# Transposing the attention probabilities: from TensorE to 32x32 blocks on VectorE

## The chip, the cores and the metric

The kernel runs on one core of one Trainium2 chip. The metric is the device time of one execution in microseconds. Three runs of the kernel before took 821.98, 822.05 and 822.8 us, median 822.05 us. The execution that the profiler recorded took 822.53 us; its span from the first to the last instruction is 820.8 us.

## What is computed

Two decoder layers over 256 positions of width 2048, with float32 inputs and outputs. Layer 0 mixes by multi-scale pooling, layer 1 by block-sparse causal attention (12 heads of 128; with 256 positions and blocks of 256 it is plain causal attention over one block). Both layers also attend over 256 memory tokens with 4 heads:

```python
s = einsum('bshd,bmhd->bhsm', q, k) * (HEAD_DIM ** -0.5)
p = softmax(s, axis=-1)
mem_o = einsum('bhsm,bmhd->bshd', p, v)
...
y = concat([branch * silu(gate_b), mem_o * silu(gate_m)]) @ w_out[i]
h = layer_norm(alpha * h + y)
```

The softmax runs along the keys. Its rows are computed with positions on the partitions and keys along the free dimension; the product with the values sums over keys, and TensorE sums over partitions. So each block of probabilities has to be transposed between the two.

## The kernel before

Every large product is split in two: each float32 operand x becomes `hi` (x in the float32r type) and `lo` (x minus hi), and a product is the sum of hi*hi, hi*lo and lo*hi. ScalarE makes the hi part (L71), VectorE the lo part (L72), in the helper `split`.

The program is one long list of items. An item is one block of weights, 128 x 1024 (512 KB), with the matmuls that consume it. `run` (L130) goes through the list: at item i it issues `prep` of item i+3 (`wh` on ScalarE, then `wl` on VectorE), then the load of item i+4 (on SP's queue), then the matmuls of item i, then whatever was registered with `later` for that item. There are four buffers of `wh`/`wl` (W_BUFS) and four of `raw` (RAW_BUFS). The engines run their queues in order, and every queue has the order in which this loop issues. A product of 256 columns is four items (`proj_t`); at the end of the fourth, `done` folds the accumulators on ScalarE and VectorE (L220, L221), and for queries and keys it adds a cast and a subtraction for each half (L228, L229).

Attention is computed for two heads at a time: `MemPair` for the memory (two pairs in each layer, 4 in all) and `MobaPair` for the causal attention (two pairs in each of three groups of four heads, 6 in all). A pair has these steps, which `plan` (L380) registers at distances in items, counted from the item that ends the query projection (called item 0 below):

- `a`: the scores on TensorE into the PSUM tile `s2`; VectorE adds the mask (causal only, L350) and takes the row maxima (L266, L267).
- `exps`, one item later: ScalarE's exponentials with row sums, into tile `p` (L271).
- `divide`, two items after `a`: the reciprocal and four multiplications by it on VectorE, in place (L275, L277).
- `b(0)` and `b(1)`, one for each head: TensorE transposes the 128x128 blocks of `p` into the PSUM tile `pt` (four blocks for the memory, L312; three for the causal pair, L362), and `split` makes `ph` and `pl` from `pt`.
- `c`: the products with the values into `o`; then `gated` (L282) multiplies by the gate and splits into `zT`, the input of the output projection.

The memory pairs use plan(1, 5, 9) and plan(7, 11, 14): item numbers of `a`, of `b(0)` and of `c`. The causal pairs use plan(1, 5, 17) and plan(7, 18, 20). Items 1 to 8 are the gate projection. In layer 1, items 9 to 16 behind the memory's gates are the keys of the first causal group; in layer 0 they are the first pooling inputs. In a causal group items 9 to 16 are the value projection.

Of the kernel before, what the change touches and what calls it, by code (L numbers as in the profile page):

```python
# [11 lines left out]
F32 = mybir.dt.float32  # L12
# [5 lines left out]
P = 128  # L18
T = 256
# [13 lines left out]
BLK = 1024  # L33
RAW_BUFS = 4
WARM = 10
SHIFT = 40
W_BUFS = 4
SHIFT = 40
LD = 4
# [6 lines left out]
def trunk(ctx: ExitStack, tc: tile.TileContext, a: dict, out: bass.AP):  # L46
    nc = tc.nc
    ctx.enter_context(tc.manual_schedule())
    sb = ctx.enter_context(tc.tile_pool(name="sb", bufs=1))
    ps = ctx.enter_context(tc.tile_pool(name="ps", bufs=1, space=bass.MemoryType.PSUM))  # L50
# [5 lines left out]
    KX = KT * 2 * T  # L56
    xT, memT = (xm[:, SHIFT + i * KX:SHIFT + (i + 1) * KX].rearrange("p (k t) -> p k t", k=KT) for i in range(2))
    kept = [xm[:, i * KX:(i + 1) * KX].rearrange("p (k n) -> p k n", k=KT) for i in range(2)]
    zT = sb.tile([P, KT, 2 * T], F32R, name="zT")
    res = sb.tile([P, 2, D], F32, name="res")  # L60
    ident = mask = psc = eps_t = stats = None

    f = lambda ap: ap.bitcast(F32)

# [1 line left out]
    def mm(o, l, r, start, stop):  # L66
        nc.tensor.matmul(o, l, r, start=start, stop=stop)  # L67

    def split(hi, lo, src):

        nc.scalar.activation(hi, src, AF.Copy)  # L71
        nc.vector.tensor_sub(lo, src, f(hi))  # L72
# [19 lines left out]
    def later(n, fn):  # L92
        events[now[0] + n].append(fn)
# [158 lines left out]
    def heads_tile(name):  # L252
        return sb.tile([P, 4, 2 * T], F32R, name=name)


    class Rows:
# [17 lines left out]
        def divide(self):  # L274
            nc.vector.reciprocal(self.sm, self.sm)  # L275
            for c, (src, dst) in enumerate(self.rows):
                nc.vector.tensor_scalar_mul(dst, dst, self.sm[:, c:c + 1])  # L277

    def gated(o, g, kt):

        zf = sb.tile([P, T], F32, name="zf", bufs=3)
        nc.vector.scalar_tensor_tensor(zf, o, 0.5, g, op0=ALU.mult, op1=ALU.mult)  # L282
        split(zT[:, kt, :T], zT[:, kt, T:], zf)

    class MemPair(Rows):
# [3 lines left out]
        def a(self):  # L289
            q, k = self.st["q"], self.st["k"]  # L290
            s = ps.tile([P, 2, 2, T], F32, name="s2")
            for j in range(2):
                h = self.h0 + j
                for t in range(2):
                    qh = q[:, h, t * P:(t + 1) * P]
                    ql = q[:, h, T + t * P:T + (t + 1) * P]
                    mm(s[:, j, t], qh, k[:, h, :T], True, False)
                    mm(s[:, j, t], qh, k[:, h, T:], False, False)
                    mm(s[:, j, t], ql, k[:, h, :T], False, True)
            self.p = p = sb.tile([P, 2, 512], F32, name="p")  # L300
            p4 = p.rearrange("p j (t m) -> p j t m", t=2)
            self.rows = [(s[:, j, t], p4[:, j, t]) for j in range(2) for t in range(2)]
            self.maxima([(0, 4, s)])

        def b(self, j):
            if j == 0:
                self.ph = sb.tile([P, 2, 512], F32R, name="ph")
                self.pl = sb.tile([P, 2, 512], F32R, name="pl")
            pt = ps.tile([P, 512], F32, name="pt")
            for m in range(2):  # L310
                for t in range(2):
                    nc.tensor.transpose(pt[:, m * T + t * P:m * T + (t + 1) * P],  # L312
                                        self.p[:, j, t * T + m * P:t * T + (m + 1) * P], ident)
            split(self.ph[:, j], self.pl[:, j], pt)

        def c(self):
            v, g = self.st["v"], self.st["g"]
# [13 lines left out]
    class MobaPair(Rows):  # L331
# [5 lines left out]
        def a(self):  # L337
            q, k = self.st["q"], self.st["k"]
            s = ps.tile([P, 2, 512], F32, name="s2")
            for j in range(2):  # L340
                h = self.h0 + j
                for t, (c0, w) in enumerate(((0, P), (P, T))):
                    qh = q[:, h, t * P:(t + 1) * P]
                    ql = q[:, h, T + t * P:T + (t + 1) * P]
                    d = s[:, j, c0:c0 + w]
                    mm(d, qh, k[:, h, :w], True, False)
                    mm(d, qh, k[:, h, T:T + w], False, False)
                    mm(d, ql, k[:, h, :w], False, True)
            self.p = p = sb.tile([P, 2, 512], F32, name="p")
            nc.vector.tensor_tensor(p[:, :, :384], s[:, :, :384],  # L350
                                    mask[:, None, :].to_broadcast([P, 2, 384]), op=ALU.add)

            self.rows = [(p[:, j, c0:c1],) * 2 for c0, c1 in ((0, P), (P, 384)) for j in range(2)]
            self.maxima([(0, 2, p[:, :, :P]), (2, 4, p[:, :, P:384])])

        def b(self, j):
            if j == 0:
                self.ph = sb.tile([P, 2, 512], F32R, name="ph")
                self.pl = sb.tile([P, 2, 512], F32R, name="pl")
            pt = ps.tile([P, 512], F32, name="pt")  # L360
            for c in range(3):
                nc.tensor.transpose(pt[:, c * P:(c + 1) * P], self.p[:, j, c * P:(c + 1) * P], ident)  # L362
            split(self.ph[:, j, :384], self.pl[:, j, :384], pt[:, :384])

        def c(self):
            v, g = self.st["v"], self.st["g"]
# [13 lines left out]
    def plan(pr, a, b, c):  # L380

        later(a, pr.a)
        later(a + 1, pr.exps)
        later(a + 2, pr.divide)
        later(b, lambda: pr.b(0))
        later(b + 1, lambda: pr.b(1))
        later(c, pr.c)
# [21 lines left out]
    def load_gb(n):  # L409
        gb = []  # L410
        for nm in ("ln_g", "ln_b"):
            tl = sb.tile([P, 512], F32, name=nm, bufs=2)
            src = a[nm][0, n * 512:(n + 1) * 512]
            nc.sync.dma_start(tl, src[None, :].to_broadcast([P, 512]))
            gb.append(tl)
        return gb
# [13 lines left out]

    def constants():

        nonlocal ident, mask, psc, eps_t, stats
        ident = sb.tile([P, P], F32, name="ident")
        mask = sb.tile([P, 384], F32, name="mask")
        psc = sb.tile([P, 12], F32, name="psc")
        eps_t = sb.tile([P, 48], F32, name="eps_t")
        stats = sb.tile([P, 2, 5, 6], F32, name="stats")
        nc.vector.memset(eps_t[:, 0:1], EPS)
        nc.scalar.dma_start(ident, a["ident"])  # L440
        nc.scalar.dma_start(mask, a["mask"])
        for g in range(2):
            inv.append(sb.tile([P, 2, T], F32, name="ln_g", bufs=2))
            nc.scalar.dma_start(inv[g], a["inv"][None, 2 * g:2 * g + 2].to_broadcast([P, 2, T]))
        nc.scalar.dma_start(psc, a["pool_scale"])

        def prepare():
            nc.vector.tensor_scalar_mul(psc, psc, 0.5)
            for z in (U0, U1, S0, S1):
                nc.vector.memset(z[:, :, :PAD], 0.0)  # L450
        later(20, prepare)
# [4 lines left out]
    def fresh(key, make):  # L456

        tiles = []

        def g():  # L460
            if not tiles:
                tiles.append(make())
                st[key] = tiles[0]
            return tiles[0]
        return g
# [16 lines left out]
    def w_in(layer, c):  # L482
        return [a["w_in"][layer, c, kb] for kb in range(4)]
# [12 lines left out]
    def mem_q_gate(layer):  # L496
        q = fresh("q", lambda: heads_tile("qq"))
        g = fresh("g", gate_tile)
        for c in range(2):
            proj_t(xT, w_in(layer, 12 + c), to_heads(q, 2 * c))  # L500
        prs = [MemPair(0, st), MemPair(2, st)]

        def go():
            plan(prs[0], 1, 5, 9)
            plan(prs[1], 7, 11, 14)
        after(go)
        for c in range(2):
            proj_t(xT, w_in(layer, 14 + c), to_gate(g, 2 * c))
# [98 lines left out]
    for half in range(2):  # L607
# [3 lines left out]
        g = fresh("g", gate_tile)  # L611
# [43 lines left out]
    for grp in range(3):  # L655
        k = fresh("k", lambda: heads_tile("kk"))
        q = fresh("q", lambda: heads_tile("qq"))
        g = fresh("g", gate_tile)
        v = fresh("v", val_tile)
        for c in range(2):  # L660
            proj_t(xT, [a["w_sk"][2 * grp + c, kb] for kb in range(4)], to_heads(k, 2 * c))
        for c in range(2):
            proj_t(xT, w_in(1, 2 * grp + c), to_heads(q, 2 * c))
        prs = [MobaPair(2 * j, 4 * grp + 2 * j, st) for j in range(2)]

        def go(prs=prs):
            plan(prs[0], 1, 5, 17)
            plan(prs[1], 7, 18, 20)
        after(go)
        for c in range(2):  # L670
            proj_t(xT, w_in(1, 6 + 2 * grp + c), to_gate(g, 2 * c))
        proj_n(xT, [a["w_sv"][grp, kb] for kb in range(8)], to_values(v), place=in_mem)
# [45 lines left out]
    def with_constants(*w):  # L718
        old(*w)
        constants()  # L720
# [71 lines left out]
    pt = ps.tile([P, 512], F32, name="pt")[:5, :P]  # L792
# [69 lines left out]
```

## Time and profile before

| | |
|---|---|
| runs | 821.98, 822.05, 822.8 us (median 822.05) |
| profiled execution | 822.53 us, span 820.8 us |
| TensorE matmul (PE) | 810.8 us busy, 99% of the span |
| TensorE weight load (PEld, beside PE) | 700.9 us, 85% |
| VectorE (DVE) | 558.5 us, 68%, 794 instructions |
| ScalarE (ACT) | 396.2 us, 48% |
| mean granted TensorE clock | 0.995 of full speed |

How to read it: an engine's busy time is the union of its instructions' time. Matmuls are pipelined, so the recorded length of one is longer than the distance from its start to the next one's start; what a group of them costs TensorE is read from the chain of work that ended last, which gives the time by which each piece moved the end on. The same holds, to a smaller degree, for VectorE and ScalarE: the recorded lengths of two neighbours overlap a little when the second needs nothing from the first.

### The profile page before, as it was taken

What the parts mean: (1) busy time and instruction counts of PE and PEld (TensorE: products, weight loads), DVE (VectorE), ACT (ScalarE), POOL (GpSimd) and SP (SyncE); (2) the same over time, 40 slices, a digit from 0 to 9 for tenths busy, and PEclk for the clock granted to TensorE, in tenths of its full rate; (3) what the DMA queues carried; (4) which work ended last, traced back from release to release, by engine and by line L of the source; (5) the groups of instructions that cost most, each with busy time, mean ns of one, the idle gap of its engine ahead of it and who ended that gap; (6) DMA issues with size and microseconds to landing.
All of it is one profiled execution on the core that took longest, in us unless ns stands there. A gap on an engine that the chain in (4) does not pass through costs nothing.

```text
span 820.8 us, 11537 instructions
## 1 busy us (share of the span) xinstructions
PE 810.8 (99%) x4446; PEld 700.9 (85%) x4446; DVE 558.5 (68%) x794; ACT 396.2 (48%) x578; POOL 0.2 (0%) x4
## 2 busy tenths in 40 slices
PE   9999999999999999999999999999999999999996
PEld 6888888898888888888888888888888888888885
DVE  5786678657956555797667667576765667658746
ACT  6564545545545343545455445354554445545520
POOL 0000000000000000000000000000000000000000
PEclk9999999999999999999999999999999999999998
DMA  8876545456557655676554544645455554636742
GB/s 319 298 250 206 170 154 192 172 181 212 185 190 278 221 186 199 201 234 201 185 170 143 193 162 163 212 159 189 177 173 170 185 187 158 224 113 233 277 132 103
DMA packets 47164, 159.15 MB, mean 194 GB/s; under 512 B 5375, under 2 KB 7167, under 8 KB 46847
## 3 DMA queue, kind: packets, MB, share of 16 engines
q1 hardware_dynamic: 45792, 155.21, 56.3%
q10 hardware_dynamic: 1316, 3.19, 1.0%
q8 instruction: 35, 0.57, 0.3%
q14 instruction: 21, 0.17, 0.1%
HBM read 156.28 MB, written 2.10 MB: 193 GB/s over the span
## 4 chain that ended last, share of the span: by engine, by line
PE 98%; DVE 1%; DMA 1%; SPq 0%; ACT 0%; issue 0%; DVEq 0%
PE acc L67 89%; PE o L67 4%; PE s L67 2%; PE pt L67 2%; DMA raw<-in_w_mk 1%; PE pt L362 0%; PE pt L312 0%; SPq L98 0%; DVE res L805 0%; PE o L637 0%; PE pt L637 0%; DVE res L786 0%; DVE wl L72 0%; ACT wh L71 0%; DVE stats L744 0%
## 5 line engine op out<-in xcount | busy, mean ns | idle before, releaser
L67 PE MATMUL acc<-xm,wh 128*128 128x512 f32 x1344 | 466.8, 394 | 0.5 <-ACT wh L71 0.5
L72 DVE TENSOR_TENSOR wl<-raw,wh 128x1024 fp32r<-128x1024 f32 (+2 forms) x250 | 295.0, 1187 | 149.8 <-ACT wh L71 148.8
L67 PE MATMUL acc<-xm,wl 128*128 128x256 f32 x1344 | 362.6, 280 | 0.1
L71 ACT ACTIVATE wh<-raw 128x1024 fp32r<-128x1024 f32 (+2 forms) x250 | 255.5, 1028 | 188.5 <-PE acc L67 131.2
L67 PEld LDWEIGHTS acc<-xm,wh 128*128 128x128 f32 x1344 | 247.2, 188 | 49.1 <-ACT wh L71 1.0
L67 PEld LDWEIGHTS acc<-xm,wl 128*128 128x128 f32 x1344 | 252.7, 188 | 7.9 <-DVE wl L72 0.9
L67 PE MATMUL acc<-wh,zT 128*128 128x512 f32 x448 | 140.0, 390 | 0.0
L67 PEld LDWEIGHTS acc<-wh,zT 128*128 128x128 f32 x448 | 84.1, 188 | 17.3
L67 PE MATMUL acc<-wl,zT 128*128 128x512 f32 x224 | 87.2, 389 | 0.0
L67 PE MATMUL acc<-xm 128*128 128x512 f32 x288 | 65.8, 389 | 0.0
L67 PEld LDWEIGHTS acc<-xm 128*128 128x128 f32 x288 | 54.1, 188 | 11.2
L72 DVE TENSOR_TENSOR xm<-raw,xm 128x1024 fp32r<-128x1024 f32 (+2 forms) x41 | 47.8, 1171 | 21.1 <-ACT xm L71 21.1
L220 ACT ACTIVATE fold<-acc 128x256 f32<-128x256 f32 x72 | 27.7, 385 | 60.8 <-PE acc L67 59.6
L71 ACT ACTIVATE xm<-raw 128x1024 fp32r<-128x1024 f32 (+2 forms) x41 | 41.3, 1014 | 19.1 <-PE acc L67 9.8
L67 PEld LDWEIGHTS acc<-wl,zT 128*128 128x128 f32 x224 | 42.1, 188 | 8.5
L221 DVE TENSOR_TENSOR fold<-acc,fold 128x256 f32<-128x256 f32 x72 | 29.5, 419 | 4.6 <-ACT fold L220 4.6
L71 ACT ACTIVATE zT<-zf 128x256 fp32r<-128x256 f32 x32 | 12.9, 414 | 39.6 <-DVE zf L282 35.4
L67 PE MATMUL acc<-xm,zT 128*128 128x256 f32 (+1 forms) x144 | 22.6, 318 | 0.0
L67 PEld LDWEIGHTS acc<-xm,zT 128*128 128x128 f32 x144 | 20.7, 190 | 1.9
L67 PE MATMUL acc<-wh,xm 128*128 128x512 f32 x64 | 21.6, 403 | 0.0
L71 ACT ACTIVATE ph<-pt 128x384 fp32r<-128x384 f32 (+1 forms) x20 | 10.7, 535 | 22.2 <-PE pt L362 13.5
L72 DVE TENSOR_TENSOR zT<-zf,zT 128x256 fp32r<-128x256 f32 x32 | 12.9, 423 | 9.7 <-ACT zT L71 9.7
(124 smaller groups left out, 504.4 us busy)
## 6 DMA issues: line engine op xcount, KB each, us to landing
raw<-in_w_in SPq DMA_DIRECT2D x128, 512.0 KB, 3.5
raw<-in_w_out SPq DMA_DIRECT2D x64, 512.0 KB, 4.1
raw<-in_w_sk SPq DMA_DIRECT2D x24, 512.0 KB, 4.4
raw<-in_w_sv SPq DMA_DIRECT2D x24, 512.0 KB, 3.3
raw<-in_w_mv SPq DMA_DIRECT2D x14, 512.0 KB, 5.2
raw<-in_w_mk SPq DMA_DIRECT2D x12, 512.0 KB, 3.4
raw<-in_xT SPq DMA_DIRECT2D x4, 512.0 KB, 4.8
res<-in_x ACTq DMA_DIRECT2D x2, 1024.0 KB, 5.4
```

The source lines that it names most:

```text
L67: nc.tensor.matmul(o, l, r, start=start, stop=stop)
L71: nc.scalar.activation(hi, src, AF.Copy)
L72: nc.vector.tensor_sub(lo, src, f(hi))
L220: nc.scalar.activation(dst, acc[:, T:], AF.Copy)
L221: nc.vector.tensor_add(dst, acc[:, :T], dst)
```

## The change

The transposes leave TensorE. `exps` writes the probabilities into a new tile `ebuf` (called `e`), in an order in which the 32x32 blocks lie as VectorE needs them: the free dimension is cut into four groups g of n blocks of 32 columns (n = 8 for a memory pair, 6 for a causal pair), and group g holds columns 32g to 32g+31 of every 128-wide block. `divide` works on `e` in place. The new method `turn(g)` issues four VectorE transposes; the one for h reads partitions 32h to 32h+31 of group g and writes partitions 32g to 32g+31 of tile `p`, at columns h*32n to (h+1)*32n. One instruction covers 32 partitions and 32n columns: 256 for a memory pair, 192 for a causal pair. `b(j)` is then only the split, from `p` in SBUF instead of from `pt` in PSUM; its operand is read in runs of 32 elements.

`plan` registers turn(0) with `divide` (item a+2, behind it), turn(1) and turn(2) at a+3, turn(3) at a+4. `b(0)` moves from item 5 to 6 in the first pairs and from 11 to 12 in the memory's second pair; that pair's `c` moves from 14 to 15. The two halves of `ebuf` take the place of the two `ln_b` buffers of the first layer norm, so that no memory is added. In the causal pairs `p` holds the masked scores until the exponentials have read them.

```diff
+        def blocks(self, n):
+            self.n = 32 * n
+            self.p = sb.tile([P, 2, 512], F32, name="p").rearrange("p j c -> p (j c)")
+            self.e = ebuf.rearrange("p j c -> p (j c)")[:, :4 * self.n]
+
+        def group(self, t, c0, c1, m):
+            t = t[:, :4 * self.n].rearrange("p (g x) -> p g x", g=4)[:, :, 32 * c0:32 * c1]
+            return t.rearrange("p g (m s) -> p m g s", m=m)
+
+        def turn(self, *groups):
+            for g in groups:
+                for h in range(4):
+                    nc.vector.transpose(self.p[32 * g:32 * g + 32, h * self.n:(h + 1) * self.n],
+                                        self.e[32 * h:32 * h + 32, g * self.n:(g + 1) * self.n])
...
 class MemPair:
-            self.p = p = sb.tile([P, 2, 512], F32, name="p")
-            p4 = p.rearrange("p j (t m) -> p j t m", t=2)
-            self.rows = [(s[:, j, t], p4[:, j, t]) for j in range(2) for t in range(2)]
+            self.blocks(8)
+            e = self.e.rearrange("p (g j m t s) -> p j t m g s", g=4, j=2, m=2, t=2)
+            self.rows = [(s[:, j, t].rearrange("p (m g s) -> p m g s", m=2, g=4), e[:, j, t])
+                         for j in range(2) for t in range(2)]
...
         def b(self, j):
-            pt = ps.tile([P, 512], F32, name="pt")
-            for m in range(2):
-                for t in range(2):
-                    nc.tensor.transpose(pt[:, m * T + t * P:m * T + (t + 1) * P],
-                                        self.p[:, j, t * T + m * P:t * T + (m + 1) * P], ident)
-            split(self.ph[:, j], self.pl[:, j], pt)
+            hi, lo = (t[:, j].rearrange("p (m h s) -> p m h s", m=4, h=4) for t in (self.ph, self.pl))
+            split(hi, lo, self.group(self.p, 4 * j, 4 * j + 4, 4))
...
 class MobaPair:
-            for c in range(3):
-                nc.tensor.transpose(pt[:, c * P:(c + 1) * P], self.p[:, j, c * P:(c + 1) * P], ident)
-            split(self.ph[:, j, :384], self.pl[:, j, :384], pt[:, :384])
+            hi, lo = (t[:, j, :384].rearrange("p (m h s) -> p m h s", m=3, h=4) for t in (self.ph, self.pl))
+            split(hi, lo, self.group(self.p, 3 * j, 3 * j + 3, 3))
...
 def plan(pr, a, b, c):
         later(a + 2, pr.divide)
+        later(a + 2, lambda: pr.turn(0))
+        later(a + 3, lambda: pr.turn(1, 2))
+        later(a + 4, lambda: pr.turn(3))
...
-            tl = sb.tile([P, 512], F32, name=nm, bufs=2)
+            tl = sb.tile([P, 512], F32, name=nm, bufs=2) if nm == "ln_g" else ebuf[:, n % 2]
...
-            plan(prs[0], 1, 5, 9)
-            plan(prs[1], 7, 11, 14)
+            plan(prs[0], 1, 6, 9)
+            plan(prs[1], 7, 12, 15)
...
-            plan(prs[0], 1, 5, 17)
+            plan(prs[0], 1, 6, 17)
             plan(prs[1], 7, 18, 20)
```

## Rows read from the trace of the kernel before

**Rows 1.** The page: busy times of the engines, and the chain that ended last by engine and by line.
```profile
PE 810.8 (99%) x4446; PEld 700.9 (85%) x4446; DVE 558.5 (68%) x794; ACT 396.2 (48%) x578; POOL 0.2 (0%) x4
...
PE 98%; DVE 1%; DMA 1%; SPq 0%; ACT 0%; issue 0%; DVEq 0%
```

**Rows 2.** All waits of TensorE (engine, line, what it waited for: us in total, times, longest).
```profile
PE pt L793 <- DVE cc L790: 2.8, 1, 2.8
PE pt L67 <- DVE zT L125: 1.2, 1, 1.2
PE acc L67 <- ACT wh L71: 0.5, 1, 0.5
PE acc L67 <- ACT cct L795: 0.4, 1, 0.4
```

**Rows 3.** The chain in order of time, memory attention of layer 1 (start us, us, what). Sixteen matmul pairs of an item are 2.78 us.
```profile
411.16 11.12 PE acc L67 x64
422.28 0.44 PE pt L312 x4
422.72 2.78 PE acc L67 x16
425.50 0.44 PE pt L312 x4
425.93 2.78 PE acc L67 x16
428.71 1.44 PE s L67 x12
430.15 5.58 PE acc L67 x32
435.72 1.44 PE o L67 x12
437.16 5.56 PE acc L67 x32
442.72 0.44 PE pt L312 x4
443.16 2.79 PE acc L67 x16
445.95 0.44 PE pt L312 x4
446.39 5.55 PE acc L67 x32
```

**Rows 4.** The same, first causal group.
```profile
496.46 0.33 PE pt L362 x3
496.79 2.78 PE acc L67 x16
```

**Rows 5.** Groups of instructions, shapes apart (count, then busy us and mean ns of one, then idle before).
```profile
L362 PE MATMUL pt<-ident,p 128*128 128x128 f32 x36 | 5.9, 271 | 0.0
L312 PE MATMUL pt<-ident,p 128*128 128x128 f32 x32 | 4.8, 272 | 0.0
L72 DVE TENSOR_TENSOR zT<-zf,zT 128x256 fp32r<-128x256 f32 x32 | 12.9, 423 | 9.7 <-ACT zT L71 9.7
L72 DVE TENSOR_TENSOR wl<-raw,wh 128x384 fp32r<-128x384 f32 x4 | 2.2, 556 | 0.6 <-ACT wh L71 0.6
L277 DVE TENSOR_SCALAR p<-p,sm 128x256 f32<-128x256 f32 x28 | 8.2, 350 | 0.1
```

**Rows 6.** VectorE in order of time, memory attention of layer 1 (start us, us, engine, line, what; in brackets the idle time before it).
```profile
406.31 0.42 DVE L221 TENSOR_TENSOR fold<-acc,fold 128x256 f32<-128x256 f32 x1
406.77 0.29 DVE L228 CAST qq<-fold 128x256 fp32r<-128x256 f32 x1
407.09 0.43 DVE L229 TENSOR_TENSOR qq<-fold,qq 128x256 fp32r<-128x256 f32 x1
407.44 0.42 DVE L221 TENSOR_TENSOR fold<-acc,fold 128x256 f32<-128x256 f32 x1
...
416.92 1.23 DVE L72 TENSOR_TENSOR wl<-raw,wh 128x1024 fp32r<-128x1024 f32 x1 [3.15 <-ACT wh L71]
418.06 0.17 DVE L275 RECIPROCAL sm<-sm 128x4 f32<-128x4 f32 x1
418.27 1.14 DVE L277 TENSOR_SCALAR p<-p,sm 128x256 f32<-128x256 f32 x4
419.32 1.22 DVE L72 TENSOR_TENSOR wl<-raw,wh 128x1024 fp32r<-128x1024 f32 x1
420.46 0.75 DVE L221 TENSOR_TENSOR fold<-acc,fold 128x256 f32<-128x256 f32 x2
421.12 1.22 DVE L72 TENSOR_TENSOR wl<-raw,wh 128x1024 fp32r<-128x1024 f32 x1
...
430.18 1.22 DVE L266 TENSOR_REDUCE nb<-s 128x4 f32<-128x1024 f32 x1 [1.41 <-PE s L67]
431.44 0.17 DVE L267 TENSOR_SCALAR nb<-nb 128x4 f32<-128x4 f32 x1
431.52 1.22 DVE L72 TENSOR_TENSOR wl<-raw,wh 128x1024 fp32r<-128x1024 f32 x1
...
437.31 0.42 DVE L282 SCALAR_TENSOR_TENSOR zf<-o,gate 128x256 f32<-128x256 f32 x1
...
439.80 0.17 DVE L275 RECIPROCAL sm<-sm 128x4 f32<-128x4 f32 x1
...
441.73 2.36 DVE L72 TENSOR_TENSOR wl<-raw,wh 128x1024 fp32r<-128x1024 f32 x2
444.00 0.69 DVE L72 TENSOR_TENSOR pl<-pt,ph 128x512 fp32r<-128x512 f32 x1
```

**Rows 7.** ScalarE in order of time, the same stage: the exponentials of the second pair, from the first to the `wh` behind them, and the one table load before the first pair's.
```profile
412.71 1.28 ACT L271 ACT_TABLE_LOAD   x1 [2.00 <-DVE nb L267]
...
433.26 0.47 ACT L271 ACTIVATE p<-s,nb 128x256 f32<-128x256 f32 x1
...
435.06 1.08 ACT L71 ACTIVATE wh<-raw 128x1024 fp32r<-128x1024 f32 x1
```

**Rows 8.** The page: issues of the load of a weight block (count, KB each, median us from issue to landing).
```profile
raw<-in_w_sk SPq DMA_DIRECT2D x24, 512.0 KB, 4.4
```

More of the change, by code (lines that the diff above doesn't have):

```diff
@@ L35 @@
 WARM = 10
-SHIFT = 40
 W_BUFS = 4
@@ L60, in trunk @@
     res = sb.tile([P, 2, D], F32, name="res")
-    ident = mask = psc = eps_t = stats = None
+    ident = mask = psc = eps_t = stats = ebuf = None
     f = lambda ap: ap.bitcast(F32)
@@ L348, in a @@
                     mm(d, ql, k[:, h, :w], False, True)
-            self.p = p = sb.tile([P, 2, 512], F32, name="p")
+            self.blocks(6)
+            p = self.p.rearrange("p (j c) -> p j c", j=2)
             nc.vector.tensor_tensor(p[:, :, :384], s[:, :, :384],
                                     mask[:, None, :].to_broadcast([P, 2, 384]), op=ALU.add)
-            self.rows = [(p[:, j, c0:c1],) * 2 for c0, c1 in ((0, P), (P, 384)) for j in range(2)]
+            self.rows = [(p[:, j, c0 * P:c1 * P].rearrange("p (m g s) -> p m g s", m=c1 - c0, g=4),
+                          self.group(self.e, 3 * j + c0, 3 * j + c1, c1 - c0))
+                         for c0, c1 in ((0, 1), (1, 3)) for j in range(2)]
             self.maxima([(0, 2, p[:, :, :P]), (2, 4, p[:, :, P:384])])
@@ L359, in b @@
                 self.pl = sb.tile([P, 2, 512], F32R, name="pl")
-            pt = ps.tile([P, 512], F32, name="pt")
-            for c in range(3):
-                nc.tensor.transpose(pt[:, c * P:(c + 1) * P], self.p[:, j, c * P:(c + 1) * P], ident)
-            split(self.ph[:, j, :384], self.pl[:, j, :384], pt[:, :384])
+            hi, lo = (t[:, j, :384].rearrange("p (m h s) -> p m h s", m=3, h=4) for t in (self.ph, self.pl))
+            split(hi, lo, self.group(self.p, 3 * j, 3 * j + 3, 3))
         def c(self):
@@ L431, in constants @@
     def constants():
-        nonlocal ident, mask, psc, eps_t, stats
+        nonlocal ident, mask, psc, eps_t, stats, ebuf
         ident = sb.tile([P, P], F32, name="ident")
@@ L438, in constants @@
         stats = sb.tile([P, 2, 5, 6], F32, name="stats")
+        ebuf = sb.tile([P, 2, 512], F32, name="ebuf")
         nc.vector.memset(eps_t[:, 0:1], EPS)
```

## The prediction

> **What bounds the kernel now.** The page first: TensorE is busy for 99% of the span and is 98% of the chain that ended last, VectorE for 68% [rows 1]. The list of TensorE's waits then shows that this is real: four waits, 4.9 us in all, at the start and the end of the program and none in an attention stage [rows 2]. So whatever leaves TensorE's queue shortens the run, as long as the other engines still deliver in time. The chain in order of time gives what leaves: four memory transposes move the end by 0.44 us, three causal ones by 0.33 us [rows 3, 4], 0.11 us each, though each is recorded with 271 ns [rows 5]. The timeline of VectorE, read last, shows how much room its queue has where the new work goes [rows 6].
>
> **What is removed.** 32 memory transposes in 8 blocks and 36 causal ones in 12 blocks [rows 5]: 8 x 0.44 + 12 x 0.33 = 7.5 us off TensorE.
>
> **What is added: the price.** Each pair issues 16 VectorE transposes, of 256 columns (4 memory pairs) or 192 (6 causal pairs). No row shows one. From below: the divisions, 256 columns each, start every 0.264 us (four last 1.14 us, one 0.35, [rows 6, 5]). The cheapest price for 192 is then 0.23. The nearest rows pass 256 columns once: 423 ns recorded [rows 5]. From 256 to 384 columns it rises by 133 ns, 1.04 ns a column, so 192 columns are 0.357 us. Two such neighbours start 0.35 us apart when the second needs nothing of the first (L229, then L221) and 0.46 when it needs it (L221, then L228) [rows 6]. From above: a second pass of the columns, 0.423 + 0.267 = 0.69 us (0.557 for 192). I take the recorded length, 0.423 and 0.357 us start to start: each transpose reads other partitions than the one ahead of it, so I give it no overlap, and since no data passes between them, no gap either. That is 64 x 0.423 + 96 x 0.357 = 61 us more for VectorE, 68% to about 75% of the span: no bound as a mean. It comes in bursts, though: turn(0) to turn(3) put 6.8 us into three items of 2.78 us in which VectorE has 1.15 us of `wl` each and more besides.
>
> [...]
>
> **What the queue does with it.** An item's `wl` is issued three items ahead, so VectorE may fall some 6 us behind before TensorE waits. I follow VectorE's queue through the memory stage of layer 1, in the clock of [rows 6]; items count from the last query item. A `wl` takes 1.15 us of the queue (start to next start) and is readable 0.1 later.
> First pair: the divisions end at 419.3, turn(0) 421.0, wl(7) and two folds 422.8, turn(1, 2) 426.2, wl(8) 427.4, turn(3) 429.0, two gate products 429.7, wl(9) 430.9 (item 9 starts at 432.06), the two `pl` with wl(10) between them 433.2, maxima 434.5 where they ended at 431.5 before [rows 6]. TensorE has not waited.
> Second pair: wl(11) and two folds to 436.3. ScalarE's exponentials wait for the maxima: 1.8 us [rows 7], then wh(12) until 437.5, so wl(12) ends at 438.6; the gated output 2.5 us (437.31 to 439.80 in [rows 6]) 441.1, reciprocal and divisions 442.4, turn(0) 444.1, gates 444.7, wl(13) 445.9. Item 13 started at 446.39 [rows 3]; four transpose blocks less, it starts at 444.63 and needs wl(13) 0.23 later: it waits 1.1 us. Then turn(1, 2) 449.3, wl(14) 450.4: item 14 waits 1.75 us. Then turn(3), wl(15) 453.3: 0.06. Then two folds with casts and subtractions (2.0 us), `pl`, wl(16), `pl` until 457.6, which `c` needs at 456.7: 0.07 and 1.03. Sum 4.0 us of waits against 1.76 us saved.
> Layer 0 has no table load ahead of its exponentials (1.28 us in layer 1, [rows 7]), so its queue is 1.3 us earlier, and plain folds at item 12: waits of 1.6 us in all against 1.76 saved.
> The causal groups: 5.7 us a pair, no gated output at item 9 and no fold at item 12. The tightest block is wl(14) (same list, 0.2 us in hand): no wait, 3 x 1.32 = 3.96 us saved.
> Sum: -7.5 + 4.0 + 1.6 = -1.8 us. The profiled execution took 822.53 us, so 820.7; it lay 0.48 us over the median of the runs, so against that 820.2.
>
> **Edits at no cost.** `b` splits from SBUF; `pl` costs the same, and `ph` waits for turn(3) in place of TensorE, behind which only `wh` queues, with three items of room. `exps` and `divide` move as many elements as before. The later `c` of the memory's second pair moves TensorE work, it adds none. Loads: SP's next load is released by the late `wl`, up to 4 us later than before, and lands 4.4 us after its issue [rows 8]; its `wh` is due another item later, so ScalarE absorbs that. `ln_b` in `ebuf` is read by the first layer norm, before the second use of `ebuf` begins. Without this cover each would show as a further wait of TensorE of 1 us or so per stage.
>
> **Rivals.**
> *The transposes overlap* like independent neighbours: 0.34 and 0.27 us. For it: no data passes between them. Against: the partitions change at every one. Until wl(13) of the second memory pair 20 transposes have each saved 0.083 us, 1.66 us, more than the 1.1 us that were missing; wl(14) is late by 0.55, the second product by 0.82, layer 0 and the causal groups wait for nothing: -7.5 + 1.4 = -6.1 us, 816.0. With every wait gone, at the bound from below, 814.6.
> *Each pays a gap as well*: the slower side. All sixteen write one tile; if each waits for the one ahead as L228 does for L221, or has a longer fixed part, they start 0.46 us apart or more (0.39 for 192). In layer 1 wl(13) is then 20 x 0.037 = 0.74 us later, wl(14) 0.3 us more: 5.2 us of waits; layer 0 2.8; and the causal wl(14) loses its margin, 0.58 in each group: 5.2 + 2.8 + 1.7 - 7.5 = +2.3, 824.4. At 0.49 and 0.42 the same list gives +6.9, 829. It decides from 0.443 us (0.375) on, where the list's sum is zero: 20 ns over my price.
> *Two passes*, 0.69 and 0.557: the burst no longer fits, and nearly every further microsecond of it is a wait; the list gives +33 us, 855. For it only that the elements are four bytes wide; against it that the other passes of [rows 5] move four bytes at one a step.
>
> [...]
>
> **Chances and range.** Forecast 0.35 (818.5 to 824 by prices of 0.41 to 0.45), overlap 0.33, gap 0.21, two passes or some other large loss 0.11. Less than 0.2% (1.65 us) can't be told from no change here. Faster: all of the overlap and somewhat over a third of the forecast's case, 0.46; within: 0.21; slower: 0.33. The range runs from the overlap's 815 to the gap's 829; only the last case and the ends lie outside.
>
> **What would show it.** TensorE's busy time falls by 7.5 us in any case, and `pt` of L312 and L362 is gone. Right: transposes recorded near 0.42 and 0.36 us, starting as the one ahead ends; waits of TensorE on `wl` (L72) at items 13 and 14 of the memory stages, 1 to 2 us each, and on `pl` in layer 1; none in the causal groups. Overlap: 0.35 us or less start to start, and hardly a wait. Gap: waits on `wl` in the causal groups too. Wrong altogether: waits elsewhere (on `ph`, on a load, on ScalarE), a lower granted clock after the waits, or a `divide` that got slower by its new order of elements.

## The result, and the profile after

The changed kernel took 830.93 us (median of four runs, 830.28 to 831.6) against 822.01 us for the kernel before on the same chip: 1.0107 of its time, 95% interval 1.0094 to 1.0119. It is slower by about 9 us, where 1.8 us faster was forecast and 829 us was the end of the range. The profiled execution's span went from 820.8 to 828.5 us.

The page of the changed kernel, the lines that answer to [rows 1]:

```profile
PE 807.3 (97%) x4378; PEld 693.8 (84%) x4378; DVE 619.5 (75%) x954; ACT 394.8 (48%) x578; POOL 0.2 (0%) x4
...
PE 77%; DVE 17%; ACT 3%; issue 2%; DMA 1%; SPq 0%; DVEq 0%
...
PE acc L66 70%; DVE p L294 6%; DVE wl L71 3%; PE o L66 3%; DVE xm L71 2%; PE pt L66 2%; ACT ebuf L270 2%; PE s L66 1%; DVE ebuf L276 1%; ACT wh L70 1%; DVE gate L241 1%; DVE pl L71 1%; DVE nb L265 1%; DMA raw<-in_w_mk 1%; DVE fold L220 0%
```

TensorE has lost its 68 transposes and is no longer the whole chain: 17% of it now runs through VectorE, the transposes (L294) being the largest part with 6%. All the line numbers are one lower than before up to the new methods (`wl` is L71, `wh` L70).

All waits of TensorE's matmuls, answering to [rows 2]; and the two waits of its weight loads that are new in size (in the kernel before weight loads waited 0.9 us for `wl`, and never for `xm`, the value weights of the causal groups):

```profile
PE acc L66 <- DVE wl L71: 7.0, 4, 2.3
PE acc L66 <- DVE xm L71: 3.9, 3, 1.3
PE pt L812 <- DVE cc L809: 2.8, 1, 2.8
PE pt L66 <- DVE zT L124: 1.2, 1, 1.2
PE acc L66 <- ACT wh L70: 0.6, 1, 0.6
PE acc L66 <- ACT cct L814: 0.4, 1, 0.4
```

```profile
PEld acc L66 <- DVE wl L71: 9.8, 8, 2.8
PEld acc L66 <- DVE xm L71: 7.0, 9, 1.7
```

The second fence is the better account. A matmul is recorded for longer than the distance to the next one's start (a matmul of 512 columns has 394 ns on the page, and the next starts 0.23 us after it), so a wait counted from its recorded end comes out short. 9.8 + 7.0 us less the 0.9 of before are 15.9 us, near what was lost: the span grew by 7.7 and 7.5 us of transposes left TensorE, 15.2 us together.

Where they fall shows in the chain's score matmuls, which open each attention stage. Kernel before, then changed kernel (start us, us, what):

```profile
76.20 1.44 PE s L67 x12
...
409.73 1.44 PE s L67 x12
...
483.95 1.38 PE s L67 x12
...
579.32 1.38 PE s L67 x12
...
674.68 1.38 PE s L67 x12
```

```profile
76.23 1.44 PE s L66 x12
...
411.71 1.44 PE s L66 x12
...
490.42 1.38 PE s L66 x12
...
586.39 1.38 PE s L66 x12
...
682.38 1.38 PE s L66 x12
```

The changed kernel is later by 0.0, 2.0, 6.5, 7.1 and 7.7 us, and by 7.7 at the end. With what each stage saved added back (1.76 us a memory stage, 1.32 a causal group), layer 0's memory stage lost 3.7 us in waits, layer 1's 6.2, the causal groups 1.9, 2.0 and 1.3.

VectorE in the memory stage of layer 1, in order of time, answering to [rows 6], and the price of a transpose from the groups by shape:

```profile
420.04 0.17 DVE L274 RECIPROCAL sm<-sm 128x4 f32<-128x4 f32 x1
420.25 1.14 DVE L276 TENSOR_SCALAR ebuf<-ebuf,sm 128x256 f32<-128x256 f32 x4
421.42 1.77 DVE L294 STREAM_TRANSPOSE p<-ebuf 32x256 f32<-32x256 f32 x4
423.23 1.23 DVE L71 TENSOR_TENSOR wl<-raw,wh 128x1024 fp32r<-128x1024 f32 x1
424.37 0.75 DVE L220 TENSOR_TENSOR fold<-acc,fold 128x256 f32<-128x256 f32 x2
425.15 3.59 DVE L294 STREAM_TRANSPOSE p<-ebuf 32x256 f32<-32x256 f32 x8
428.77 1.23 DVE L71 TENSOR_TENSOR wl<-raw,wh 128x1024 fp32r<-128x1024 f32 x1
430.03 1.80 DVE L294 STREAM_TRANSPOSE p<-ebuf 32x256 f32<-32x256 f32 x4
...
447.88 1.22 DVE L71 TENSOR_TENSOR wl<-raw,wh 128x1024 fp32r<-128x1024 f32 x1
449.13 3.59 DVE L294 STREAM_TRANSPOSE p<-ebuf 32x256 f32<-32x256 f32 x8
452.75 1.23 DVE L71 TENSOR_TENSOR wl<-raw,wh 128x1024 fp32r<-128x1024 f32 x1
```

```profile
L294 DVE STREAM_TRANSPOSE p<-ebuf 32x192 f32<-32x192 f32 x96 | 35.5, 370 | 1.6
L294 DVE STREAM_TRANSPOSE p<-ebuf 32x256 f32<-32x256 f32 x64 | 27.9, 436 | 1.1
```

Eight transposes last 3.59 us: each starts 0.45 us after the one ahead, recorded 0.436 us, so the next begins 0.013 us after the last has ended. There is also a seam, an overlap lost, at both ends of a turn: the division before turn(0) and the transpose before `wl` each run out in full (420.25 + 1.14 = 421.39, next start 421.42; 421.42 + 1.77 = 423.19, next start 423.23), where `wl` and a fold overlap by 0.09 us (423.23 + 1.23 = 424.46, next start 424.37).

### The profile page after: what moved, and what is told of

Its sections match the earlier page's. It is cut to its first block, busy times and chain, and to the rows that moved or that the text cites. A ratio compares the mean times of both kernels' runs of the same rounds, so it can differ in the third digit from the quotient of the medians.

```text
span 828.5 us, 11566 instructions
## 1 busy us (share of the span) xinstructions
PE 807.3 (97%) x4378; PEld 693.8 (84%) x4378; DVE 619.5 (75%) x954; ACT 394.8 (48%) x578; POOL 0.2 (0%) x4
## 4 chain that ended last, share of the span: by engine, by line
PE 77%; DVE 17%; ACT 3%; issue 2%; DMA 1%; SPq 0%; DVEq 0%
PE acc L66 70%; DVE p L294 6%; DVE wl L71 3%; PE o L66 3%; DVE xm L71 2%; PE pt L66 2%; ACT ebuf L270 2%; PE s L66 1%; DVE ebuf L276 1%; ACT wh L70 1%; DVE gate L241 1%; DVE pl L71 1%; DVE nb L265 1%; DMA raw<-in_w_mk 1%; DVE fold L220 0%
## 5 line engine op out<-in xcount | busy, mean ns | idle before, releaser
L71 DVE TENSOR_TENSOR wl<-raw,wh 128x1024 fp32r<-128x1024 f32 (+2 forms) x250 | 294.9, 1187 | 139.0 <-ACT wh L70 138.0
L70 ACT ACTIVATE wh<-raw 128x1024 fp32r<-128x1024 f32 (+2 forms) x250 | 255.0, 1028 | 198.9 <-PE acc L66 130.0
L66 PEld LDWEIGHTS acc<-xm,wl 128*128 128x128 f32 x1344 | 253.5, 189 | 16.8 <-DVE wl L71 9.8
L66 PE MATMUL acc<-xm 128*128 128x512 f32 x288 | 67.9, 394 | 3.9 <-DVE xm L71 3.9
L294 DVE STREAM_TRANSPOSE p<-ebuf 32x192 f32<-32x192 f32 (+1 forms) x160 | 63.4, 396 | 2.7
L71 DVE TENSOR_TENSOR xm<-raw,xm 128x1024 fp32r<-128x1024 f32 (+2 forms) x41 | 47.7, 1169 | 11.6 <-ACT xm L70 11.4
L70 ACT ACTIVATE xm<-raw 128x1024 fp32r<-128x1024 f32 (+2 forms) x41 | 41.1, 1011 | 16.3 <-PE acc L66 6.6
L70 ACT ACTIVATE zT<-zf 128x256 fp32r<-128x256 f32 x32 | 12.9, 415 | 37.9 <-DVE zf L300 33.6
L70 ACT ACTIVATE ph<-p 128x384 fp32r<-128x384 f32 (+1 forms) x20 | 11.1, 557 | 39.5 <-DVE p L294 39.5
```

The source lines that it names most:

```text
L294: nc.vector.transpose(self.p[32 * g:32 * g + 32, h * self.n:(h + 1) * self.n], self.e[32 * h:32 * h + 32, g * self.n:(g + 1) * self.n])
```

## The experiments

The theory after the result: the amount of work that VectorE got is affordable, its place is not. The turns lie in front of `wl` in VectorE's queue, in bursts that its lead of three items can't cover, and a transpose costs 0.45 us because it changes the quarter of partitions. Rivals: the new layouts and the split from SBUF cost the time; a transpose costs what it costs wherever it reads; VectorE has too much to do as a whole.

**The transposes left out.** `turn` does nothing, and the splits read `e`.

```diff
-            for g in groups:
-                for h in range(4):
-                    nc.vector.transpose(self.p[32 * g:32 * g + 32, h * self.n:(h + 1) * self.n],
-                                        self.e[32 * h:32 * h + 32, g * self.n:(g + 1) * self.n])
+            pass
...
-            split(hi, lo, self.group(self.p, 4 * j, 4 * j + 4, 4))
+            split(hi, lo, self.group(self.e, 4 * j, 4 * j + 4, 4))
...
-            split(hi, lo, self.group(self.p, 3 * j, 3 * j + 3, 3))
+            split(hi, lo, self.group(self.e, 3 * j, 3 * j + 3, 3))
```

> Leaves out the VectorE transposes; the splits read tile e, all else as in the changed kernel (so the probabilities go untransposed into the products). Queue theory (the whole loss is VectorE time in front of wl): no wait of TensorE in the attention stages, the 7.5 us of TensorE transposes gained in full, 814.5 us. Rival (the new order of elements in exps and divide, the split from SBUF, or the shared ebuf cost the time): divide or exps longer per instruction and a good part of the loss stays, 820 us or more.

Measured: 814.52 us, ratio 0.9907 (0.989 to 0.9923): 7.7 us gained on the 822.23 us of the kernel before in this comparison. Divisions of 256 columns take as long as before (350 ns, [rows 5]):

```profile
L276 DVE TENSOR_SCALAR ebuf<-ebuf,sm 128x256 f32<-128x256 f32 x28 | 8.2, 348 | 0.1
```

The split's `ph` of 512 columns takes 617 ns on ScalarE (599 before), and no matmul waits for anything between 60 and 730 us. So the edits around the transposes cost no run time, and the 7.5 us of TensorE time were really there.

**No change of quarter between most of them.** A quarter is a group of 32 partitions, starting at partition 0, 32, 64 or 96. Each transpose reads the partitions that it writes.

```diff
-                                        self.e[32 * h:32 * h + 32, g * self.n:(g + 1) * self.n])
+                                        self.e[32 * g:32 * g + 32, h * self.n:(h + 1) * self.n])
```

> The sixteen transposes of a pair stay, of the same sizes, but each reads the same 32 partitions that it writes, so that the quarter changes only every fourth one (blocks are not moved to other partitions). Theory that the change of partitions forbids overlap: three of four start 0.35 us (0.28 for 192 columns) after the one ahead instead of 0.449 (0.385), and by the queue's list most waits go: 816 to 818 us. Rival (a transpose simply takes 0.449 from start to start, wherever it reads): still 0.449, still 829 to 831 us.

Measured: 818.02 us, ratio 0.9949 (0.9934 to 0.9964). VectorE, memory stage of layer 1, second pair, turn(0) and turn(1, 2):

```profile
440.44 1.42 DVE L294 STREAM_TRANSPOSE p<-ebuf 32x256 f32<-32x256 f32 x4
443.66 2.84 DVE L294 STREAM_TRANSPOSE p<-ebuf 32x256 f32<-32x256 f32 x8
```

Eight take 2.84 us where they took 3.59: about 0.35 us from start to start. 160 instructions of the same sizes, a tenth of a microsecond less each, and 13 us of run time less. Waits of 1.5 us for `wl` and 0.8 for `pl` are left, all in the memory stages. The time lies at the upper end of what was expected, it follows the queue, and the rival with a fixed price falls.

The seams can be read here too. First pair, turn(0) and the `wl` behind it:

```profile
416.92 1.14 DVE L276 TENSOR_SCALAR ebuf<-ebuf,sm 128x256 f32<-128x256 f32 x4
418.10 1.41 DVE L294 STREAM_TRANSPOSE p<-ebuf 32x256 f32<-32x256 f32 x4
419.45 1.17 DVE L71 TENSOR_TENSOR wl<-raw,wh 128x1024 fp32r<-128x1024 f32 x1
```

This turn stays in the first quarter, where `wl` starts as well, and `wl` overlaps it again by 0.06 us; behind turn(3), which ends in the last quarter, the next instruction still starts 0.03 us after the end. So in these traces the seam behind a turn goes with the change of quarter. The seam in front of turn(0) stays (0.04 us between the last division and the first transpose), though no quarter changes there; turn(0) reads what the divisions have just written, and that may be its reason.

**Which side's change it is.** Four orders of quarters in the four groups of a pair; the blocks are not the right ones.

```diff
-                for h in range(4):
-                    nc.vector.transpose(self.p[32 * g:32 * g + 32, h * self.n:(h + 1) * self.n],
-                                        self.e[32 * h:32 * h + 32, g * self.n:(g + 1) * self.n])
...
+            order = (((0, 0, 0), (0, 0, 1), (0, 0, 2), (0, 0, 3)),
+                     ((0, 1, 0), (1, 1, 1), (2, 1, 2), (3, 1, 3)),
+                     ((2, 2, 0), (2, 3, 0), (2, 2, 1), (2, 3, 1)),
+                     ((0, 2, 2), (1, 3, 2), (2, 2, 3), (3, 3, 3)))
...
+                for r, w, c in order[g]:
+                    nc.vector.transpose(self.p[32 * w:32 * w + 32, c * self.n:(c + 1) * self.n],
+                                        self.e[32 * r:32 * r + 32, g * self.n:(g + 1) * self.n])
```

> The sixteen transposes of a pair in four orders of quarters, one for each of the four groups (which blocks are read and written is wrong for the result): group 0 reads and writes quarter 0 throughout, in group 1 only the quarter read changes, in group 2 only the quarter written, in group 3 both. If a change on either side is what forbids the overlap: 0.35 us start to start in group 0 (256 columns), 0.45 in the other three. If only the side read matters: group 2 at 0.35 too; only the side written: group 1. The recorded length is 0.436 in all if it holds no waiting.

Measured, a single run: 825.34 us. VectorE in layer 0, first pair: group 0, groups 1 and 2, group 3.

```profile
84.57 1.41 DVE L298 STREAM_TRANSPOSE p<-ebuf 32x256 f32<-32x256 f32 x4
...
87.78 3.58 DVE L298 STREAM_TRANSPOSE p<-ebuf 32x256 f32<-32x256 f32 x8
...
92.66 1.79 DVE L298 STREAM_TRANSPOSE p<-ebuf 32x256 f32<-32x256 f32 x4
```

Group 0, which stays in one quarter, takes 1.41 us for four, the others 1.79 each, groups 1 and 2 alike. A change on either side alone is enough, and a change on both costs no more: 0.45 us from start to start with a change of either kind, 0.35 without one. One part of the expectation missed: the recorded length is not 0.436 us throughout. In group 0 the first transpose is recorded with 0.43 us and the three behind it with 0.39.

**One stage at a time.** The causal pairs alone on VectorE, and the memory pairs alone (the same edit with `MemPair`); the others go back to TensorE with the old plan and the old `a` and `b`.

```diff
+        if isinstance(pr, MobaPair):
+            later(a + 2, lambda: pr.turn(0))
+            later(a + 3, lambda: pr.turn(1, 2))
+            later(a + 4, lambda: pr.turn(3))
```

> Only the causal pairs use VectorE, with the plan of the changed kernel; the memory pairs are as before, transposed by TensorE, with plan(1, 5, 9) and (7, 11, 14). If the stages' losses add up: three groups at +0.6 us each as read from the two traces, 823.8 us. If the memory stage's lateness was carried into the causal groups: these gain their 1.3 us each, 818 us.

> Only the memory pairs use VectorE, with the plan of the changed kernel; the causal pairs are as before. If the losses add up: layer 0 +2.0, layer 1 +4.5, 828.5 us, with the granted clock at about half in a stretch of some 3 us behind the waits of layer 1. If they don't: between 822 and 825 us.

Measured: 824.36 us (ratio 1.0027, 1.0017 to 1.0036) and 828.66 us (1.0081, 1.0066 to 1.0096) against 822.23: +2.1 and +6.4, together +8.5 where the whole change gave +8.9. The losses add up stage by stage. Both kinds of stage lose more than they save, the memory stages most of it. The slow stretch expected in layer 1 of the second kernel came too, and is taken up in the next part.

**The clock.** In layer 1 TensorE's granted clock fell behind the two waits. Stretch 454 to 458 us of the changed kernel (busy times and counts by engine, then granted clock, DMA share, GB/s):

```profile
454.00:458.00 4.00, 3.97 (x14) 3.45 (x15) 3.86 (x8) 2.17 (x4) 0.00 (x0) 0.57 0.40 131
```

From 454.5 to 457.5 us the granted clock is 0.50 of full speed; pairs of matmuls (512 and 256 columns) started 0.64 us apart there instead of 0.35, five of them, 1.5 us. Two starts of TensorE:

```profile
454.67 0.63 PE L66 MATMUL acc<-xm,wh 128*128 128x512 f32 x1
...
455.31 0.63 PE L66 MATMUL acc<-xm,wh 128*128 128x512 f32 x1
```

This kernel fills the two waits with matmuls that nobody reads.

```diff
+            def fill(n):
+                o = ps.tile([P, 512], F32, name="pt")
+                for _ in range(n):
+                    mm(o, xT[:, 0, :P], xT[:, 0], True, True)
+            if layer == 1:
+                later(12, lambda: fill(8))
+                later(13, lambda: fill(8))
```

> The changed kernel, with eight matmuls of 128x512 whose result nobody reads behind items 12 and 13 of the memory stage of layer 1, where TensorE waits 2.3 and 1.8 us for wl. Clock theory (the granted clock falls to half because TensorE has stood still, and the slow stretch costs 1.5 us): the waits are filled, the clock stays at 1.0 behind them and the time falls by some 1.5 us, 829.4 us. Rival (the slow stretch has another cause): clock at half as before and 831 us or a little more.

Measured: 830.49 us, ratio 1.0103 (1.0087 to 1.0118), span 828.5 us as without it. The same stretch, and the line of TensorE's waits for `pl`:

```profile
454.00:458.00 4.00, 3.96 (x21) 3.16 (x21) 3.83 (x9) 2.04 (x4) 0.00 (x0) 1.00 0.42 131
```

```profile
PE o L66 <- DVE pl L71: 0.8, 1, 0.8
```

The first half of the expectation holds: with the two waits filled the granted clock of the stretch is 1.00 where it was 0.57. The second half misses: 0.4 us less than the changed kernel, inside the spread of either's runs. The time came back as other waits, for one of 0.8 us for `pl` at `c`, which the forecast had listed and the changed kernel did not show. In that stretch VectorE is the bound (busy 3.83 to 3.86 of the 4 us in both kernels), and TensorE's slow three microseconds lay beside its work.

When the clock falls isn't settled. The kernel with the memory pairs alone has the same first wait of 2.3 us, and there the clock fell behind that one already, where the changed kernel kept it. Stretch 450 to 454 us, memory pairs alone and changed kernel:

```profile
450.00:454.00 4.00, 3.75 (x13) 2.88 (x13) 3.87 (x8) 0.00 (x0) 0.00 (x0) 0.58 0.38 126
```

```profile
450.00:454.00 4.00, 2.21 (x13) 1.68 (x11) 3.86 (x8) 0.00 (x0) 0.00 (x0) 1.00 0.40 131
```

**Spread out.** The same instructions, one turn an item, the second pairs later.

```diff
-        later(a + 2, lambda: pr.turn(0))
-        later(a + 3, lambda: pr.turn(1, 2))
-        later(a + 4, lambda: pr.turn(3))
+        for g in range(4):
+            later(a + 2 + g, lambda g=g: pr.turn(g))
...
-            plan(prs[0], 1, 6, 9)
-            plan(prs[1], 7, 12, 15)
+            plan(prs[0], 1, 8, 11)
+            plan(prs[1], 11, 18, 21)
...
-            plan(prs[0], 1, 6, 17)
-            plan(prs[1], 7, 18, 20)
+            plan(prs[0], 1, 8, 17)
+            plan(prs[1], 9, 18, 20)
```

> The same VectorE work as in the changed kernel, one turn an item instead of three items with one, two and one, and the second pair later: memory plan(1, 8, 11) and (11, 18, 21), causal plan(1, 8, 17) and (9, 18, 20). If the loss came from the burst and not from the amount: VectorE busy 619 us as now, no wait of TensorE over 0.4 us, 814.5 to 815.5 us, faster than both kernels. If the amount is too much for VectorE: the waits move to later items, 820 us or more.

Measured: 816.48 us, ratio 0.9929 (0.9917 to 0.9941). VectorE is as busy as in the changed kernel, and of the waits two of 0.7 us are left. Page, and waits of TensorE:

```profile
PE 804.2 (99%) x4378; PEld 693.6 (85%) x4378; DVE 619.0 (76%) x954; ACT 395.8 (49%) x578; POOL 0.2 (0%) x4
```

```profile
PE o L66 <- DVE pl L71: 0.7, 1, 0.7
PE acc L66 <- DVE wl L71: 0.7, 1, 0.7
```

14.5 us less than the changed kernel with the same work: the amount is not the cause. The time is 1 us above what was expected; two waits of 0.7 us were not expected. The edit does two things at once, one turn an item and later steps for the pairs (the memory's second pair starts at item 11 instead of 7, the causal one at 9); which of the two gave how much was not separated. The next kernel changes the turns alone.

**All in one burst** (against the changed kernel), and **the spread stretched further** (against the spread kernel):

```diff
-        later(a + 2, lambda: pr.turn(0))
-        later(a + 3, lambda: pr.turn(1, 2))
-        later(a + 4, lambda: pr.turn(3))
+        later(a + 2, lambda: pr.turn(0, 1, 2, 3))
```

```diff
-    def plan(pr, a, b, c):
+    def plan(pr, a, b, c, at=None):
...
-            later(a + 2 + g, lambda g=g: pr.turn(g))
+            later(a + (at or (2, 3, 4, 5))[g], lambda g=g: pr.turn(g))
...
-            plan(prs[1], 11, 18, 21)
+            plan(prs[1], 11, 19, 22, (2, 3, 6, 7))
```

> The opposite of the spread: all sixteen transposes of a pair behind divide, in one item; amount, price and all other item numbers as in the changed kernel. If the burst sets the loss: the wl behind it comes 7 us later than its turn in one piece, waits of 3 to 5 us in each pair, 843 us (VectorE's queue followed item by item gives 20 us over the kernel before). If only the amount counts: 831 us as the changed kernel.

> e_spread with the memory's second pair stretched: turns at items 13, 14, 17 and 18 (they pass by the heads' folds of item 16 in layer 1), b at 19 and 20, c at 22. If the two waits left in e_spread (0.7 us each, for pl in layer 0 and wl in layer 1) came from the same queue: both gone, 815 us. If they have another cause: 816.5 us as e_spread.

Measured: 854.5 us (ratio 1.0391, 1.0377 to 1.0405) and 814.89 us (0.9912, 0.9898 to 0.9925). The burst, VectorE in the memory stage of layer 1, second pair, and the waits of its weight loads:

```profile
450.21 7.18 DVE L294 STREAM_TRANSPOSE p<-ebuf 32x256 f32<-32x256 f32 x16
457.42 0.76 DVE L241 SCALAR_TENSOR_TENSOR gate<-th,fold 128x256 f32<-128x256 f32 x2
458.10 3.49 DVE L71 TENSOR_TENSOR wl<-raw,wh 128x1024 fp32r<-128x1024 f32 x3
```

```profile
PEld acc L66 <- DVE wl L71: 18.7, 10, 5.1
PEld acc L66 <- DVE xm L71: 10.9, 3, 3.6
```

One piece of 7.18 us, and behind it three `wl` that had piled up. The waits, 29.6 us less the 7.5 saved, give 22 us, near the 20 of the queue followed by hand; but the span grew by 31, and the run takes 11.5 us more than the 843 expected. The mean granted clock over the run is 0.979 against 0.995 before. In the parts of the span that hold the five attention stages it is 0.94 (70 to 130 us), 0.94 (410 to 470), 0.97 (470 to 580), 0.98 (580 to 690) and 0.96 (690 to 851, the end of the program included), and 1.00 in the others. Behind the waits of layer 1's memory stage it falls in this stretch:

```profile
460.00:464.00 4.00, 4.00 (x14) 3.38 (x14) 3.86 (x9) 0.31 (x1) 0.00 (x0) 0.52 0.88 258
```

It holds 14 matmuls; 458 to 462 us of the changed kernel, at full clock, hold 28. The remaining 9 us may lie in the parts at a lower clock; that is not shown, for no kernel was run that fills the waits.

In the stretched spread no matmul waits for more than 0.3 us in an attention stage; the two waits are gone, as expected. It takes within 0.4 us of the kernel without any transposes, and is the fastest of those that do them, 7.4 us ahead of the kernel before and 16 us ahead of the change as made.

## Why the prediction was wrong

What leaves TensorE: right. 7.5 us, shown by the kernel without transposes (7.7 us gained).

The price on VectorE: this step failed, in two terms, the price of one transpose and the seams. "I take the recorded length, 0.423 and 0.357 us start to start", with no overlap and no gap. The recorded lengths are 0.436 and 0.370, with 0.013 us between two: 0.449 and 0.385. That lies past the 0.443 and 0.375 at which the forecast's own list turns from gain to loss. Giving no overlap was right, and the reason offered, the change of partitions, is what the kernel with four orders shows (0.45 us with it, 0.35 without). The price of the first rival, 0.34, is near that of transposes that stay in a quarter, 0.35.

This term alone does not carry the time out of the range. 0.449 lies inside the 0.41 to 0.45 that the forecast had allowed itself, and by its list (zero at 0.443 and 0.375, +2.3 us at 0.46 and 0.39) the measured price gives some +1.2 us, about 823 us, an estimate.

The other term was put at nothing without a reason: the seams. From the first reciprocal to the end of the first pair's turn(3) the list had 11.0 us (418.06 to 429.0); it took 11.8 (420.04 to 431.83). Sixteen times 0.026 is 0.4; the other 0.4 is some 0.13 us for each of the three turns, whose neighbours no longer overlap with them. The forecast's own reading, that a change of partitions leaves no overlap, holds for these neighbours too (except the division ahead of turn(0)) and was not applied to them.

What the queue does with it: right in kind and in place, wrong in size. Item 13 of layer 1 was to wait 1.1 us; to the end of wl(13) VectorE needed 29.1 us from the first reciprocal instead of 27.8, and item 13 waited 2.3. Item 14 was to wait 1.75 and waited 1.8 by its matmul. Layer 0's stage was to wait 1.6 us in all and lost 3.7. In the causal groups "no wait" rested on 0.2 us in hand at wl(14): 28 transposes and five turns' seams use it up and 1.2 us more, and 1.3 to 2.0 were lost in a group. The sum of the waits was forecast at 5.6 us and came to 15.2. An estimate from the same figures: price and seams add 1.6 us to each memory stage (32 transposes, six turns) and 1.2 to each causal group, about half of it each, which makes some 12.4; the other 2.8 us, more than half of them in the causal groups, no run explains. (The terms of the forecast's sum, as printed, add up to -1.9 us and not -1.8; nothing hangs on it.)

The second rival, a gap at each transpose, came nearest in its outcome, waits in the causal groups included, and its 0.21 was too small a chance: the forecast's price stood 20 ns under the turning point, with the seams left out, and all that was uncertain about the price could only add to it except the overlap. Its first reason is refuted: the sixteen write one tile in the kernel without changes of quarter too, and start 0.35 us apart there. What there is of a gap is 0.013 us and a recorded length 0.013 us above the forecast's. Its figures were low as well (824.4 at 0.46 us, 829 at 0.49), since it had no seams either; price and seams together are about 0.475 us a transpose, by its list some 827.

Edits at no cost: right, all of them (the kernel without transposes). The third rival, two passes, is out: the 0.436 us recorded for 256 columns is near the forecast's 0.423 for one pass and far from the 0.69 of this rival.

The feature that was to mean "wrong altogether", a lower clock after the waits, appeared, and the kernel with filled waits was only 0.4 us faster, inside the spread; it was not what went wrong.

## What to carry to other kernels

Work moved to an engine with spare time on average has to be placed by that engine's queue: list what it does item by item between the moved pieces and the operand that the bound engine needs next, and spread the pieces until each fits into its item. Here the same 160 instructions gave 854.5, 830.9, 816.5 or 814.9 us, by where they and the steps around them stood. When the list's margin is a few tenths of a microsecond, the overlap lost at the borders of the moved pieces belongs in it (some 0.13 us for each of the first pair's three turns here), and a spread version is worth a run before the change is judged.

## What was not expected

A VectorE transpose that reads or writes another quarter of the partitions than the one ahead of it cost 0.1 us more here, start to start (0.45 against 0.35 us at 256 columns). Behind a turn that ends in another quarter, 0.04 us of gap stood where `wl` and a fold overlap by 0.09.

TensorE's granted clock fell to 0.50 of full speed after it had stood still for 2.3 and then 1.8 us; with the same gaps filled by unread matmuls it was 1.00. It did not fall in layer 0, where the waits were 1.0 and 1.8 us (1.00 from 98 to 122 us). With the memory pairs alone it fell after the wait of 2.3 us by itself (0.58 from 450 to 454 us), so these runs give no rule for when it falls. In the changed kernel the fall did not lengthen the run, because VectorE was the bound in that stretch (busy for 3.86 of the 4 us).

The changed kernel's matmul records understate its waits: TensorE's matmuls show 10.9 us of waits for `wl` and `xm`, its weight loads 16.8, and the weight loads' sum is the one that comes near the 15.2 us lost.
